# Regrouping the short matrix products of a chunked recurrence on TensorE

## The chip, the cores and the metric

The kernel runs on one core of one Trainium2 chip. The metric is the device time of one execution in microseconds (us); several runs of the same program are taken and their median is quoted. A profiled execution of the same program gives the trace.

## What is computed

One decoder layer over 256 tokens with a model width of 2048, all in f32:

```
h = rmsnorm(x);  u = h @ w_in          # ten column groups: c b xa za | q f iv og | ga gb
ya = b * conv3(c * xa) * silu(za)      # short convolution branch, 1024 wide
o  = hgrn2_chunked(silu(q), (1-lb)*sigmoid(-f), iv, log_f)   # 8 heads of 128
yb = rmsnorm_per_head(o) * silu(og)
m  = sigmoid(ga) * (ya @ w_a) + sigmoid(gb) * (yb @ w_b);  x = x + m @ w_o
x  = x + sigmoid(rmsnorm(x) @ w_pg) * (p @ w_pp);  out = rmsnorm(x)
```

The recurrence keeps a decaying state per head. For query time t and key time s <= t its weight is `sum_k q[t,k] * exp(B[t,k] - B[s,k]) * key[s,k]`, where B is the running sum of log_f. The result is these weights times the values `iv`.

## The kernel before, in words

**The main products.** The weights come from memory in chunks of 256 x 512 elements. Each chunk is split on the chip into a rounded half `whi` (ScalarE, ACT, line 124) and a remainder `wlo` (VectorE, DVE, line 125), and TensorE (PE) multiplies activations with them in three passes: 12 products of 128 x 128 by 512 columns per chunk (line 937, function `product`). There are four pairs of buffers `whi`/`wlo`, and the loop at line 940 splits up to four chunks ahead of the chunk being multiplied, so the split of chunk n waits until the products of chunk n-4 are done. Chunks are numbered from 0: 4 for `w_pp`, then 8 for each half of f, q, iv, og, c, xa, za, b, and so on.

**The epilogues.** What follows each group of columns is a Python generator. The main loop calls `advance()` once per chunk, which runs every active generator up to its next `yield`. A `yield` therefore puts what comes after it one chunk later. The program order of each engine is the order in which these pieces are issued, apart from small moves by the scheduler.

**The recurrence.** `hgrn(j)` (line 351) is such a generator, started once for each half j of the heads (4 heads of 128 channels) after the `og` columns. It covers 256 times as two blocks of 128, the second one held in reversed time order. In each block the 128 x 128 weights are built by levels: for block size B in `LEVELS = [128, 64, 32, 16, 8, 4]` the keys of one half of each block of B times meet the queries of the other half, with the decay split at the half's border. `level(B)` makes the decay factors with two subtractions (DVE and GpSimd), two exponentials (ACT), and `combine` makes the operand tile X with four multiplications (two on DVE, two on GpSimd, line 418). Then come:

- `products(bk, key, query, B)` (line 385): for each head, products on PE that use only a strip of the array's columns (`tile_position`). `quarters(B)` gives the strips: two of 64 rows for level 128, four of 32 rows for the others. They are f32, and each product is two instructions in the trace.
- `keep(dst, mask, src, B)` (line 394): masked copies (COPY_PREDICATED, line 396) from PSUM into the tile `both`, one for each strip.

Levels go two by two through two PSUM banks: products of two levels, then two yields, then the copies. After the third pair come the operands of the link between the two blocks (line 475 on), of the diagonal pairs (lines 488 to 501), and two masked copies of `both` into `a[:, 0]` and `a[:, 1]` (line 502). Then, in one burst on PE, the link `bo` (line 512, two strips of 64 rows, 128 columns) and the diagonal pairs of both blocks (line 519, through `products` with B = 2). Two chunks later DVE copies `bo` to `aoff` (line 522) and keeps the diagonals with four masked copies for each block (line 524); one chunk later PE multiplies `a` and `aoff` by the values (lines 529 to 532: 12 products of 128 x 128 by 128 columns, two instructions each).

So each half has five bursts of short products on PE among the main products: three of levels, one of link and diagonals, and the product with the values.

**The end.** `last_norm(1)` (line 756) scales the last 128 rows of the output in five pieces (DVE lines 770 and 776, ACT line 774) and sends each with a DMA (line 777), four of them from SyncE's queue (SP) and one from ACT's.

Of the kernel before, what the change touches and what calls it, by code (L numbers as in the profile page):

```python
# [11 lines left out]
AF = mybir.ActivationFunctionType  # L12
ALU = mybir.AluOpType
PSUM = bass.MemoryType.PSUM

P = 128
# [7 lines left out]
CW = 512  # L24
# [6 lines left out]
LEVELS = [128, 64, 32, 16, 8, 4]  # L31
# [13 lines left out]
def hybrid_kernel(ctx, tc, xT, x, pT, prm, gfin, masks, w_in, w_a, w_b, w_o, w_pg, w_pp, out):  # L45
    nc = tc.nc
# [124 lines left out]
    mask_t = const.tile([P, len(LEVELS) + 4, P], mybir.dt.int32, name="mask_t")  # L171
# [45 lines left out]
    def spread(ap, t):  # L217

        return ap.rearrange("p (b c t e) -> p t c b e", b=4, c=4, t=NT)[:, t]
# [128 lines left out]
    def hgrn(j):  # L351
# [9 lines left out]
        def new_X():  # L361

            n, made[0] = made[0], made[0] + 1
            X = t4("X", 2) if n % 4 < 2 else pools["branch"].tile(
                [P, 1024], F32, tag=f"ybT{'hl'[n % 2]}{j}", bufs=1, name=nm("X")
            )
            return X.rearrange("p (w h t) -> p w h t", w=2, h=4)

        a = tmp.tile([P, 2, 4, P], F32, tag="a", bufs=1, name=nm("a"))
        nc.gpsimd.memset(a, 0.0)  # L370
        both = tmp.tile([P, 4, P], F32, tag="both", bufs=1, name=nm("both"))
        nc.gpsimd.memset(both, 0.0)
        aoff = tmp.tile([P, 4, P], F32, tag="aoff", bufs=1, name=nm("aoff"))

        def heads(ap):
            return ap.rearrange("p (h t) -> p h t", h=4)

        def quarters(B):

            n = max(B // 2, 32)  # L380
            for r in range(P // n):
                c = r ^ 1 if B >= 64 else r
                yield slice(r * n, (r + 1) * n), slice(c * n, (c + 1) * n)

        def products(bk, key, query, B):

            for h in range(4):
                for r, c in quarters(B):
                    nc.tensor.matmul(  # L389
                        heads(bk)[r, h, c], key(h)[:, r], query(h)[:, c], start=True, stop=True,  # L390
                        tile_position=(0, r.start),
                    )

        def keep(dst, mask, src, B):
            for r, c in quarters(B):
                nc.vector.copy_predicated(  # L396
                    out=dst[r, :, c], data=src[r, :, c],
                    mask=mask_t[r, mask : mask + 1, c].to_broadcast([r.stop - r.start, 4, c.stop - c.start]),
                )

        def halves(ap, B):
            r = ap.rearrange("p (n two h) -> p n two h", two=2, h=B // 2)
            return r[:, :, 0, :], r[:, :, 1, :]
# [20 lines left out]
        def level(B):  # L424

            n, h = 1024 // B, B // 2
            e = t4()
            bl, br = halves(b, B)
            el, er = halves(e, B)
            if B > SCAN:  # L430
                nc.scalar.activation(out=el, in_=halves(y, B)[0], func=AF.Exp, scale=-1.0)
                nc.scalar.activation(out=er, in_=br, func=AF.Exp)
            else:
                ref = bl[:, :, h - 1 : h].to_broadcast([P, n, h])
                nc.vector.tensor_tensor(out=el, in0=bl, in1=ref, op=ALU.subtract)
                nc.gpsimd.tensor_tensor(out=er, in0=br, in1=ref, op=ALU.subtract)  # L436
                nc.scalar.activation(out=el, in_=el, func=AF.Exp, scale=-1.0)
                nc.scalar.activation(out=er, in_=er, func=AF.Exp)
            return combine(e, B)
# [4 lines left out]
            out=y.rearrange("p (n c) -> p n c", c=SCAN), in0=b.rearrange("p (n c) -> p n c", c=SCAN),  # L444
            in1=tot.rearrange("p (n o) -> p n o", o=1).to_broadcast([P, 16, SCAN]), op=ALU.subtract,
        )
        yield
        Xs = [level(LEVELS[0])]
        yield
        yield  # L450
        Xs.append(level(LEVELS[1]))
        yield
        yield
        yield

        for i in range(0, len(LEVELS), 2):
            bks = [bank("s") for _ in range(2)]
            for n, X in enumerate(Xs):
                products(bks[n], lambda h: X[:, 0, h, :], lambda h: X[:, 1, h, :], LEVELS[i + n])
            more = i + 2 < len(LEVELS)  # L460
            Xs = [level(LEVELS[i + 2])] if more else []
            yield
            yield
            for n, bk in enumerate(bks):
                keep(both, i + n, heads(bk), LEVELS[i + n])
            if more:
                Xs.append(level(LEVELS[i + 3]))
                yield
                yield
                yield  # L470

        e = t4()
        el, er = halves(e, P)
# [2 lines left out]
            out=el, in0=yl,  # L476
            in1=tot.rearrange("p (n s) -> p n s", s=2)[:, :, 1:2].to_broadcast([P, 8, SCAN]), op=ALU.subtract,
# [3 lines left out]
        X = new_X()  # L481
# [7 lines left out]
            out=f.rearrange("p (n c) -> p n c", c=1), in0=br, in1=bl, op=ALU.subtract  # L489
# [8 lines left out]
        for blk in range(2):  # L498
            kk, qq = k2[:, :, blk, :, 1 - blk, 0], q2[:, :, blk, :, 1 - blk, 0]
# [3 lines left out]
                out=a[:, blk],  # L503
                mask=mask_t[:, len(LEVELS) + blk : len(LEVELS) + blk + 1, :].to_broadcast([P, 4, P]), data=both,
# [2 lines left out]
        yield  # L507
        bo = bank("s")
        for h in range(4):
            for r in range(2):  # L510
                rows = slice(r * 64, (r + 1) * 64)
                nc.tensor.matmul(
                    heads(bo)[rows, h, :], X[:, 0, h, rows], X[:, 1, h, :], start=True, stop=True,
                    tile_position=(0, r * 64),
                )
        bk = [bank("s") for _ in range(2)]
        for blk in range(2):
            kk, qq = (z.rearrange("p (h k t) -> p h k t", h=4, k=2)[:, :, blk, :] for z in (kT, qT))
            products(bk[blk], lambda h: kk[:, h, :], lambda h: qq[:, h, :], 2)
        yield  # L520
        yield
        nc.vector.tensor_copy(out=aoff.rearrange("p h t -> p (h t)"), in_=bo)
        for blk in range(2):
            keep(a[:, blk], len(LEVELS) + 2 + blk, heads(bk[blk]), 2)
        yield
        o = [bank("s") for _ in range(2)]
        for h in range(4):
# [9 lines left out]
        for n in range(8):  # L537
            t, h = n // 4, n % 4
            if n == 4:
                yield  # L540
            nc.scalar.activation(
                out=sq[:, n * P : (n + 1) * P], in_=o[t][:, h * P : (h + 1) * P], func=AF.Square,
                scale=state["rstd1"][:, t : t + 1], accum_out=ss[:, n : n + 1],
            )
        for t in range(NT):
            s = slice(t * CW, (t + 1) * CW)
# [4 lines left out]
        for n in range(8):  # L551
            t, h = n // 4, n % 4
            if n == 4:
                yield
            nc.scalar.activation(
                out=spread(sq, t)[:, h], in_=yb[:, n * P : (n + 1) * P].rearrange("p (b e) -> p b e", e=32),
                func=AF.Identity, scale=rh[:, n : n + 1],
# [198 lines left out]
    def last_norm(t):  # L756

        xs, r, tot = state["x"], sc(1, "r3", 2), state["tot3", t]
        nc.vector.tensor_tensor(out=tot, in0=tot, in1=state["ss3"][:, t * 6 + 4 : t * 6 + 5], op=ALU.add)
        nc.gpsimd.tensor_tensor(out=r, in0=tot, in1=mhalf[:, :1], op=ALU.pow)  # L760
        n = CW // 2

        for eng, q0, q1, queue in (
            (nc.vector, 4, 5, nc.sync), (nc.vector, 5, 6, nc.sync), (nc.scalar, 0, 2, nc.sync),
            (nc.vector, 6, 8, nc.sync), (nc.scalar, 2, 4, nc.scalar),
        ):
            s = slice(q0 * n, q1 * n)
            d = xs[:, t, s]
            if q0 >= 6:
                nc.vector.scalar_tensor_tensor(  # L770
                    out=d, in0=d, scalar=r, in1=state["gfin"][:, s], op0=ALU.mult, op1=ALU.mult
                )
            elif eng is nc.scalar:
                nc.scalar.activation(out=d, in_=d, func=AF.Identity, scale=r)
            else:
                nc.vector.tensor_scalar(out=d, in0=d, scalar1=r, scalar2=None, op0=ALU.mult)
            queue.dma_start(out=out[:, t, s], in_=d)

    def ep_last(t, halves):

# [159 lines left out]
    for pos, (gi, c) in enumerate(steps[:last_group]):  # L940
        kind, j, w, g, opname = groups[gi]
# [35 lines left out]
        for i in range(2):  # L977
            k = 2 * c + i
            s = slice(i * CW, (i + 1) * CW)
# [41 lines left out]
    for t, halves in ((0, (0, 1)), (1, (0,)), (1, (1,))):  # L1021
        bk, n = bank("g"), CW // 2
        for c in range(nlast):
# [4 lines left out]
            for i in range(2):  # L1028
                k = 2 * c + i
                s = slice(i * CW + halves[0] * n, i * CW + (halves[-1] + 1) * n)  # L1030
# [85 lines left out]
```

## Time and profile before

| what | value |
|---|---|
| median of 3 runs | 831.42 us (831.42 to 831.85) |
| the profiled execution's own time | 831.84 us |
| its span in the trace | 830.1 us |
| PE busy (main and short products) | 816.9 us, 98% |
| DVE, ACT, GpSimd busy | 538.3, 430.9, 84.8 us |
| mean granted TensorE clock | 0.996 |

The trace gives each instruction's start and duration by engine and line. Matmuls are pipelined, so a PE row's duration overlaps with the next one's; the time that a product takes from the others is read from the distance between starts. Bursts of the first half lie between 123 and 186 us of the span, those of the second half between 307 and 370 us.

### The profile page before, as it was taken

Reading aid. Unit: us, or ns where it says so; the run is one execution under the profiler, and the core shown is the slowest. Engines: PE = TensorE matmul, PEld = TensorE weight load, DVE = VectorE, ACT = ScalarE, POOL = GpSimd, SP = SyncE. Lnnn points to the kernel's source line nnn. Section 1 sums busy time; section 2 is a strip of 40 time slices with the busy share of each in tenths; the row PEclk is TensorE's granted clock in tenths of the full one; section 3 lists DMA queues with packets and bytes.
Section 4 is the critical chain, followed back from the end, with each engine's and each line's share of the span. In section 5 each row is a group of like instructions: output and inputs, shape, how many; then the busy total and the mean of one; then the engine's idle time right before and its main releaser. Section 6 shows DMA issues by size and latency. Waiting matters only on the chain.

```text
span 830.1 us, 10589 instructions
## 1 busy us (share of the span) xinstructions
PE 816.9 (98%) x4122; PEld 674.3 (81%) x4122; DVE 538.3 (65%) x662; ACT 430.9 (52%) x553; POOL 84.8 (10%) x74
## 2 busy tenths in 40 slices
PE   9999999999999999999999999999999999999995
PEld 6888888878888888878888888888888888888885
DVE  6746678896866588896745545545645656679633
ACT  7666565446564465455544443443444455566522
POOL 1000035110000054100001001000100000001210
PEclk9999999999999999999999999999999999999998
DMA  9969655647876554657655755755655787987702
GB/s 341 372 256 340 222 193 197 204 153 219 277 235 232 203 203 152 204 192 241 227 203 172 254 189 196 253 203 191 231 191 198 253 281 246 330 304 269 293 0 103
DMA packets 40947, 187.25 MB, mean 226 GB/s; under 512 B 4672, under 2 KB 14400, under 8 KB 22720
## 3 DMA queue, kind: packets, MB, share of 16 engines
q1 hardware_dynamic: 40464, 185.78, 64.7%
q10 hardware_dynamic: 432, 0.79, 0.3%
q8 instruction: 32, 0.52, 0.3%
q14 instruction: 19, 0.16, 0.1%
HBM read 172.92 MB, written 13.63 MB: 225 GB/s over the span
## 4 chain that ended last, share of the span: by engine, by line
PE 93%; DVE 3%; issue 2%; ACT 1%; POOLq 0%; POOL 0%; DVEq 0%
PE g L937 91%; DVE wlo L125 1%; PE s L389 1%; PE s L937 1%; PE s L817 1%; DVE t L264 0%; PE s L531 0%; PE s L529 0%; DVE a L396 0%; ACT whi L124 0%; DVE both L396 0%; DVE X L483 0%; PE s L530 0%; DVE t L492 0%; DVE t L494 0%
## 5 line engine op out<-in xcount | busy, mean ns | idle before, releaser
L125 DVE TENSOR_TENSOR wlo<-raw,whi 128x1024 fp32r<-128x1024 f32 (+1 forms) x293 | 360.4, 1235 | 251.8 <-ACT whi L124 250.8
L124 ACT ACTIVATE whi<-raw 128x1024 fp32r<-128x1024 f32 (+1 forms) x293 | 307.6, 1056 | 323.6 <-PE g L937 279.4
L937 PE MATMUL g<-whi,xh 128*128 128x512 f32 (+1 forms) x912 | 352.0, 387 | 0.0
L937 PE MATMUL g<-whi,xl 128*128 128x512 f32 (+1 forms) x912 | 351.8, 386 | 0.0
L937 PE MATMUL g<-wlo,xh 128*128 128x512 f32 (+1 forms) x912 | 351.7, 386 | 0.0
L937 PEld LDWEIGHTS g<-whi,xh 128*128 128x128 f32 x912 | 171.3, 188 | 34.6
L937 PEld LDWEIGHTS g<-whi,xl 128*128 128x128 f32 x912 | 171.3, 188 | 34.3
L937 PEld LDWEIGHTS g<-wlo,xh 128*128 128x128 f32 x912 | 171.4, 188 | 33.9
L937 PE MATMUL g<-whi,mh 128*128 128x512 f32 x128 | 49.8, 390 | 0.0
L937 PE MATMUL g<-wlo,mh 128*128 128x512 f32 x128 | 49.7, 389 | 0.0
L937 PE MATMUL g<-whi,ml 128*128 128x512 f32 x128 | 49.6, 390 | 0.0
L659 POOL TENSOR_TENSOR t<-ga,gb 128x512 f32<-128x512 f32 x6 | 10.6, 1786 | 195.8 <-DVE gb L654 195.8
L937 PE MATMUL g<-whi,yaTh 128*128 128x512 f32 x72 | 28.3, 399 | 0.0
L937 PEld LDWEIGHTS g<-whi,mh 128*128 128x128 f32 x128 | 24.0, 188 | 5.3 <-ACT mh L665 0.3
L937 PE MATMUL g<-whi,yaTl 128*128 128x512 f32 x72 | 28.3, 396 | 0.0
L937 PEld LDWEIGHTS g<-whi,ml 128*128 128x128 f32 x128 | 23.9, 188 | 5.1 <-DVE ml L666 0.2
L937 PEld LDWEIGHTS g<-wlo,mh 128*128 128x128 f32 x128 | 24.0, 188 | 5.0
L937 PE MATMUL g<-wlo,yaTh 128*128 128x512 f32 x72 | 27.9, 390 | 0.0
L436 POOL TENSOR_TENSOR t<-b 128x512 f32<-128x512 f32 x10 | 18.9, 1890 | 67.0 <-DVE b L319 38.7
L937 PE MATMUL g<-whi,ybTh 128*128 128x512 f32 x64 | 24.9, 389 | 0.0
L937 PE MATMUL g<-whi,ybTl 128*128 128x512 f32 x64 | 24.9, 389 | 0.0
L937 PE MATMUL g<-wlo,ybTh 128*128 128x512 f32 x64 | 24.9, 389 | 0.0
(154 smaller groups left out, 522.4 us busy)
## 6 DMA issues: line engine op xcount, KB each, us to landing
raw<-in_w_in SPq DMA_DIRECT2D x93, 1024.0 KB, 5.0
raw<-in_w_o SPq DMA_DIRECT2D x16, 1024.0 KB, 5.5
raw<-in_w_pg SPq DMA_DIRECT2D x16, 1024.0 KB, 5.8
turn<-t SPq DMA_DIRECT2D x72, 128.0 KB, 2.7
t<-turn SPq DMA_DIRECT2D x18, 512.0 KB, 4.9
raw<-in_w_a SPq DMA_DIRECT2D x8, 1024.0 KB, 5.0
raw<-in_w_b SPq DMA_DIRECT2D x8, 1024.0 KB, 5.0
raw<-in_w_in SPq DMA_DIRECT2D x6, 512.0 KB, 8.3
```

The lines of the kernel that those rows point to most:

```text
L124: a = nc.scalar.activation(out=hi[:, s], in_=src[:, s], func=AF.Copy)
L125: v = nc.vector.tensor_tensor(out=lo[:, s], in0=src[:, s], in1=hi[:, s].bitcast(F32), op=ALU.subtract)
L389: nc.tensor.matmul(heads(bk)[r, h, c], key(h)[:, r], query(h)[:, c], start=True, stop=True, tile_position=(0, r.start),)
L436: nc.gpsimd.tensor_tensor(out=er, in0=br, in1=ref, op=ALU.subtract)
L659: (nc.vector if j == 3 else nc.gpsimd).tensor_tensor(out=spread(m, t), in0=blocks(ga[:, s]), in1=blocks(gb[:, s]), op=ALU.add)
L817: nc.tensor.matmul(wb, warm[:, :P], warm, start=True, stop=True)
L937: nc.tensor.matmul(psum, a, b, start=first and n == 0, stop=last and n == 2)
```

## The change

- `quarters(B)` now yields four strips of 32 rows at every level; level 128 has 64 columns in each.
- The narrow levels 32, 16, 8, 4 are made first. Their products go in one burst into one PSUM bank, level i at columns 32*i of each head's 128. Four masked copies of the full 128 x 512 follow, each reading its 32 columns repeated over the four column blocks.
- The wide levels 128 and 64 are made after that burst. Their products are issued with the link and the diagonals, in the same bank as the first block's diagonal; the second block's diagonal takes 32 columns of another bank.
- The link's products use four strips of 32 rows instead of two of 64, and its copy `aoff` goes from DVE to ACT.
- The two masks for the shared bank are put together from the loaded ones by four small DVE instructions in the first half.
- Three masked copies of 128 x 512 take the place of the eight after the diagonals. There are two yields in place of one before the product with the values. In all, the product with the values of each half stands one chunk earlier than before (behind chunk 60 in place of three products into chunk 62 in the first half, by the built program).
- `last_norm` works in four pieces of 512 columns in place of five.

```diff
         def quarters(B):
-            n = max(B // 2, 32)
-            for r in range(P // n):
-                c = r ^ 1 if B >= 64 else r
-                yield slice(r * n, (r + 1) * n), slice(c * n, (c + 1) * n)
-
-        def products(bk, key, query, B):
+            for r in range(0, P, 32):
+                c = {128: (r // 64 ^ 1) * 64, 64: r ^ 32}.get(B, r)
+                n = max(B // 2, 32)
+                yield slice(r, r + 32), slice(c, c + n)
+
+        def products(bk, key, query, B, at=None):
             for h in range(4):
                 for r, c in quarters(B):
                     nc.tensor.matmul(
-                        heads(bk)[r, h, c], key(h)[:, r], query(h)[:, c], start=True, stop=True,
-                        tile_position=(0, r.start),
+                        heads(bk)[r, h, c if at is None else slice(at, at + 32)], key(h)[:, r], query(h)[:, c],
+                        start=True, stop=True, tile_position=(0, r.start),
                     )
-        def keep(dst, mask, src, B):
-            for r, c in quarters(B):
+        def keep(dst, mask, src, at=None):
+            if at is None:
                 nc.vector.copy_predicated(
-                    out=dst[r, :, c], data=src[r, :, c],
-                    mask=mask_t[r, mask : mask + 1, c].to_broadcast([r.stop - r.start, 4, c.stop - c.start]),
+                    out=dst, data=src, mask=mask_t[:, mask : mask + 1, :].to_broadcast([P, 4, P])
                 )
+                return
+            n = P // 32
+            nc.vector.copy_predicated(
+                out=dst.rearrange("p h (n c) -> p h n c", n=n),
+                data=src[:, :, at : at + 32].rearrange("p h (n c) -> p h n c", n=1).to_broadcast([P, 4, n, 32]),
+                mask=mask_t[:, mask : mask + 1, :].rearrange("p h (n c) -> p h n c", n=n).to_broadcast([P, 4, n, 32]),
+            )
...
         yield
-        Xs = [level(LEVELS[0])]
-        yield
-        yield
-        Xs.append(level(LEVELS[1]))
-        yield
-        yield
-        yield
-
-        for i in range(0, len(LEVELS), 2):
-            bks = [bank("s") for _ in range(2)]
-            for n, X in enumerate(Xs):
-                products(bks[n], lambda h: X[:, 0, h, :], lambda h: X[:, 1, h, :], LEVELS[i + n])
-            more = i + 2 < len(LEVELS)
-            Xs = [level(LEVELS[i + 2])] if more else []
+        if j == 0:
+            m = lambda i: mask_t[:, i, :]
+            for out, a0, a1, op in ((0, 0, 1, ALU.max), (1, 0, 7, ALU.mult), (0, 0, 6, ALU.mult), (0, 0, 8, ALU.max)):
+                nc.vector.tensor_tensor(out=m(out), in0=m(a0), in1=m(a1), op=op)
+        Xs = []
+        for i in range(2, len(LEVELS)):
+            Xs.append(level(LEVELS[i]))
             yield
             yield
-            for n, bk in enumerate(bks):
-                keep(both, i + n, heads(bk), LEVELS[i + n])
-            if more:
-                Xs.append(level(LEVELS[i + 3]))
+            if i % 2:
                 yield
-                yield
-                yield
+        bk = bank("s")
+        for i, X in enumerate(Xs):
+            products(bk, lambda h: X[:, 0, h, :], lambda h: X[:, 1, h, :], LEVELS[2 + i], 32 * i)
+        Xs = [level(LEVELS[0])]
+        yield
+        yield
+        for i in range(4):
+            keep(both, 2 + i, heads(bk), 32 * i)
+        Xs.append(level(LEVELS[1]))
+        yield
+        yield
+        yield
...
         bo = bank("s")
         for h in range(4):
-            for r in range(2):
-                rows = slice(r * 64, (r + 1) * 64)
+            for r in range(0, P, 32):
                 nc.tensor.matmul(
-                    heads(bo)[rows, h, :], X[:, 0, h, rows], X[:, 1, h, :], start=True, stop=True,
-                    tile_position=(0, r * 64),
+                    heads(bo)[r : r + 32, h, :], X[:, 0, h, r : r + 32], X[:, 1, h, :], start=True, stop=True,
+                    tile_position=(0, r),
                 )
         bk = [bank("s") for _ in range(2)]
+        for i, X in enumerate(Xs):
+            products(bk[0], lambda h: X[:, 0, h, :], lambda h: X[:, 1, h, :], LEVELS[i])
         for blk in range(2):
             kk, qq = (z.rearrange("p (h k t) -> p h k t", h=4, k=2)[:, :, blk, :] for z in (kT, qT))
-            products(bk[blk], lambda h: kk[:, h, :], lambda h: qq[:, h, :], 2)
-        yield
-        yield
-        nc.vector.tensor_copy(out=aoff.rearrange("p h t -> p (h t)"), in_=bo)
-        for blk in range(2):
-            keep(a[:, blk], len(LEVELS) + 2 + blk, heads(bk[blk]), 2)
+            products(bk[blk], lambda h: kk[:, h, :], lambda h: qq[:, h, :], 2, 0 if blk else None)
+        yield
+        yield
+        nc.scalar.activation(out=aoff.rearrange("p h t -> p (h t)"), in_=bo, func=AF.Copy)
+        keep(a[:, 0], 0, heads(bk[0]))
+        keep(a[:, 1], 1, heads(bk[0]))
+        keep(a[:, 1], len(LEVELS) + 3, heads(bk[1]), 0)
+        yield
         yield
...
     def last_norm(t):
-        n = CW // 2
-        for eng, q0, q1, queue in (
-            (nc.vector, 4, 5, nc.sync), (nc.vector, 5, 6, nc.sync), (nc.scalar, 0, 2, nc.sync),
-            (nc.vector, 6, 8, nc.sync), (nc.scalar, 2, 4, nc.scalar),
-        ):
-            s = slice(q0 * n, q1 * n)
+        for q in (2, 0, 3, 1):
+            s = slice(q * CW, (q + 1) * CW)
             d = xs[:, t, s]
...
-            queue.dma_start(out=out[:, t, s], in_=d)
+            (nc.scalar if q == 1 else nc.sync).dma_start(out=out[:, t, s], in_=d)
```

More of the change, by code (lines that the diff above doesn't have):

```diff
@@ L760, in last_norm @@
         nc.gpsimd.tensor_tensor(out=r, in0=tot, in1=mhalf[:, :1], op=ALU.pow)
-        n = CW // 2
-        for eng, q0, q1, queue in (
-            (nc.vector, 4, 5, nc.sync), (nc.vector, 5, 6, nc.sync), (nc.scalar, 0, 2, nc.sync),
-            (nc.vector, 6, 8, nc.sync), (nc.scalar, 2, 4, nc.scalar),
-        ):
-            s = slice(q0 * n, q1 * n)
-            d = xs[:, t, s]
-            if q0 >= 6:
+        for q in (2, 0, 3, 1):
+            s = slice(q * CW, (q + 1) * CW)
+            d = xs[:, t, s]
+            if q < 2:
+                nc.scalar.activation(out=d, in_=d, func=AF.Identity, scale=r)
+            elif q == 2:
+                nc.vector.tensor_scalar(out=d, in0=d, scalar1=r, scalar2=None, op0=ALU.mult)
+            else:
                 nc.vector.scalar_tensor_tensor(
@@ L772, in last_norm @@
                 )
[L773 to L777, printed above, removed]
+            (nc.scalar if q == 1 else nc.sync).dma_start(out=out[:, t, s], in_=d)
     def ep_last(t, halves):
```

## The prediction

> **What bounds the kernel now.** I read the page first, then the waits of PE, then the chain of work that ended last.
>
> ```profile
> span 830.1 us, 10589 instructions
> PE 816.9 (98%) x4122; PEld 674.3 (81%) x4122; DVE 538.3 (65%) x662; ACT 430.9 (52%) x553; POOL 84.8 (10%) x74
> ...
> PE 93%; DVE 3%; issue 2%; ACT 1%; POOLq 0%; POOL 0%; DVEq 0%
> ...
> L125 DVE TENSOR_TENSOR wlo<-raw,whi 128x1024 fp32r<-128x1024 f32 (+1 forms) x293 | 360.4, 1235 | 251.8 <-ACT whi L124 250.8
> L124 ACT ACTIVATE whi<-raw 128x1024 fp32r<-128x1024 f32 (+1 forms) x293 | 307.6, 1056 | 323.6 <-PE g L937 279.4
> ```
> ```profile
> PE s L529 <- DVE a L396: 2.6, 2, 1.3
> ```
> ```profile
> 185.35 121.77 PE g L937 x537
> ```
>
> PE is the bound: it is 98% busy and makes 93% of the chain. The splits on ACT and DVE wait for it (279.4 us of ACT's idle time), not it for them. In the second fence, once the kernel runs, PE waits for another engine in one place only, the product with the values (line 529), once for each half. The third row gives the pace: 121.77 us for 537 products, 0.227 us each. So whatever is taken out of PE's stream between two main products comes off the end, one for one, as long as nothing else becomes late. What counts is how much longer than 0.227 us the main products stand apart around the short ones.
>
> **The bursts.** The timeline of PE in the first half, one block for the first pair of levels, one for the second, the ends of one for the third, one for link and diagonals, one for the product with the values (columns: start, length, what, count):
>
> ```profile
> 123.05 0.39 PE L937 MATMUL g<-whi,xl 128*128 128x512 f32 x1
> 123.37 1.07 PE L389 MATMUL s<-X 128*64 128x64 f32 x48
> 124.37 0.50 PE L937 MATMUL g<-whi,xh 128*128 128x512 f32 x1
> 124.71 0.40 PE L937 MATMUL g<-wlo,xh 128*128 128x512 f32 x1
> ...
> 137.86 0.39 PE L937 MATMUL g<-whi,xl 128*128 128x512 f32 x1
> 138.18 0.77 PE L389 MATMUL s<-X 128*32 128x32 f32 x64
> 139.21 0.40 PE L937 MATMUL g<-wlo,xh 128*128 128x512 f32 x1
> ...
> 152.40 0.39 PE L937 MATMUL g<-whi,xl 128*128 128x512 f32 x1
> ...
> 153.75 0.40 PE L937 MATMUL g<-wlo,xh 128*128 128x512 f32 x1
> ...
> 169.66 0.39 PE L937 MATMUL g<-whi,xl 128*128 128x512 f32 x1
> 169.98 1.09 PE L512 MATMUL s<-X 128*64 128x128 f32 x16
> 171.00 0.76 PE L389 MATMUL s<-qT,kT 128*32 128x32 f32 x64
> 171.70 0.50 PE L937 MATMUL g<-whi,xh 128*128 128x512 f32 x1
> 172.03 0.40 PE L937 MATMUL g<-wlo,xh 128*128 128x512 f32 x1
> ...
> 180.44 0.39 PE L937 MATMUL g<-whi,xl 128*128 128x512 f32 x1
> 182.13 0.46 PE L529 MATMUL s<-v,a 128*128 128x128 f32 x2 [1.30 <-DVE a L396]
> 184.06 0.39 PE L530 MATMUL s<-v,aoff 128*128 128x128 f32 x2
> 184.29 0.39 PE L531 MATMUL s<-v,a 128*128 128x128 f32 x2
> 185.10 0.48 PE L937 MATMUL g<-whi,xh 128*128 128x512 f32 x1
> 185.42 0.40 PE L937 MATMUL g<-wlo,xh 128*128 128x512 f32 x1
> ```
>
> The first main product after a burst also holds up the second (0.34 us), so I measure from the last main product before to the second one after, less two paces (0.453 us). Burst 1 costs 1.66 - 0.453 = 1.21 us, burst 2 1.35 - 0.453 = 0.90, burst 3 (levels 8 and 4) 0.90, link with diagonals 2.37 - 0.453 = 1.92: together 4.92 us a half. The product with the values costs 4.98 - 0.453 = 4.53.
>
> How much of it is work? Two narrow windows inside bursts 2 and 1:
>
> ```profile
> 138.24 0.39 PE L389 MATMUL s<-X 128*32 128x32 f32 x25
> ```
> ```profile
> 123.48 0.40 PE L389 MATMUL s<-X 128*64 128x64 f32 x7
> ```
>
> A row's length runs to the end of its last instruction, and one lasts about 0.2 us here, so 25 instructions of 32 columns start within 0.2 us: 0.0079 us each. Those of level 128 start 7 in 0.18 us: 0.029 us each. Burst 2 is then 64 x 0.0079 = 0.51 us of work and 0.39 us of entering and leaving. That 0.39 is what a removed burst saves. Changing the strip's width inside a burst costs too: burst 1 is 0.39 + 32 x 0.0079 + 16 x 0.029 = 1.10, 0.11 under what it took.
>
> After the change a half has burst A, four narrow levels: 128 x 0.0079 + 0.39 = 1.40 us. Burst B has link, wide levels and diagonals. Its work is that of burst 4 (1.92, entering and leaving included) and of burst 1 without its fixed part (1.21 - 0.39 = 0.82): 2.74 us with both changes of width kept, about 2.50 if these vanish because all strips are now 32 wide. The unknown is a strip of 32 with long rows, which this trace does not hold: level 128 and the link become 32 instructions each in place of 16. I take four strips side by side at half the cost of two, as the 32-column rows run (0.0079 against 0.029 for twice the columns and twice the width, near a quarter). So A and B are 3.90 to 4.14 against 4.92: 0.8 to 1.0 us saved a half, and I take 1.0. The bound above is no gain from four strips over two, 16 more instructions of each kind at today's cost: 16 x 0.029 = 0.46 for the level, and for the link 16 x 0.055 = 0.88 (its 16 take 1.02 us before the diagonals start, less the change of width). The bound below is the short rows' 0.0079 for all 64, some 0.8 us cheaper; that would need rows two and four times as long to cost nothing, so I leave it out.
>
> The Trainium skill speaks against many small products: "TensorE: Matmul & The Clock Gate", in the section that asks why 56 ns and not 53.3, says that starts never come closer than about 25 ns however few the columns. By it the 32 added instructions would cost 0.8 us a half and the sum would be 827.7 us. The row with 25 starts in 0.2 us does not agree: separate strips start three times closer than that, so I give this case no chance of its own.
>
> **The wait before the product with the values.** Its clean cost is 24 instructions at 0.111 us (two rows of x2 stand 0.23 us apart), 2.68 us, and 0.09 us on each side (the burst's first start comes 0.32 after a main product in place of 0.227): 2.86 us. The other 1.67 of the 4.53 us is waiting, mostly the 1.46 us from 180.67 to 182.13. What ended it, from DVE's timeline:
>
> ```profile
> 177.72 1.41 DVE L264 SCALAR_TENSOR_TENSOR t<-g,r1s,t 128x512 f32<-128x512 f32 x2
> 179.04 1.22 DVE L125 TENSOR_TENSOR wlo<-raw,whi 128x1024 fp32r<-128x1024 f32 x1
> 180.18 0.69 DVE L522 COPY aoff<-s 128x512 f32<-128x512 f32 x1
> 180.78 2.46 DVE L396 COPY_PREDICATED a<-mask_t,s 32x128 f32<-32x128 int32 x8
> ```
>
> The copies stand behind the split of chunk 63, the product with the values three products into chunk 62. Split 63 cannot begin before product 59 ends. From there two chunks and three products (6.1 us) hold a split (1.06 + 1.23), `aoff` (0.6) and the copies (2.46), 0.8 us to spare, and the `za` work on line 264 (1.41) in front of the split eats it.
>
> In the built program the three copies stand behind the split of chunk 61 and the product with the values behind chunk 60. Split 61 can begin when product 57 ends, three chunks (8.2 us) ahead. In that time DVE needs the split's 2.3 us, the copies and one convolution step (0.35). The `za` work now follows them, and `aoff` is on ACT, behind split 61 and in front of split 62. For the copies:
>
> ```profile
> L396 DVE COPY_PREDICATED both<-mask_t,s 32x128 f32<-32x128 int32 x40 | 12.0, 299 | 0.8
> L396 DVE COPY_PREDICATED a<-mask_t,s 32x128 f32<-32x128 int32 x16 | 4.7, 294 | 0.2
> L502 DVE COPY_PREDICATED a<-mask_t,both 128x512 f32<-128x512 int32 x4 | 3.0, 762 | 0.0
> L396 DVE COPY_PREDICATED both<-mask_t,s 64x256 f32<-64x256 int32 x4 | 1.8, 446 | 0.0
> ```
>
> From 128 to 256 columns a copy grows by 0.147 us, so 512 cost about 0.75, which the row of line 502 confirms. Three of them make 2.3 us. Of 8.2 us 3.3 are left, so the wait goes: 1.67 us a half. DVE as a whole gets lighter: (12.0 + 4.7 + 1.8) / 2 = 9.3 us of copies a half become 7 x 0.76 = 5.3, and `aoff` leaves it. The four mask instructions (128 columns each, about 0.3 us, once) come early, where split buffers are four chunks deep. Repeated reading of 32 columns in PSUM is a pattern not in this trace; I price it by its 512 columns, and bound it by twice that. At 1.5 us a copy DVE would reach the diagonal's keys 3 us later. By my walk along its queue they are ready 1.8 us before burst B wants them, so PE would wait 1.2 us a half. What is late next is DVE still: level 128 reuses the buffer of level 32, so its multiplications wait for burst A; the splits behind them are for chunks that PE reaches three chunks later.
>
> **The end.**
>
> ```profile
> 823.52 0.62 DVE L776 TENSOR_SCALAR xs<-xs,r 128x256 f32<-128x256 f32 x2 [0.67 <-POOL r L760]
> 823.90 2.06 SPq L777 DMA_DIRECT2D out<-xs  x4
> ```
>
> SP issues four DMAs about 0.55 us apart ((2.06 - 0.41) / 3, the last lasting 0.41), the last at 825.55. With one piece for the first two, the first leaves 0.27 us later (when 0.62 us of scaling is done) and the last of three at 824.17 + 1.10 = 825.27, 0.28 us earlier. If the transfers set the end it is up to 0.27 later. I take 0.15 earlier.
>
> **The sum.** 2 x (1.0 + 1.67) + 0.15 = 5.5 us. Against the profiled execution's own 831.84 us (span 830.1 and 1.7 around it) that gives 826.3 us; against the median of 831.42 it gives 825.9. I predict 826.1 us.
>
> **The rivals.**
> - *The wait stays.* DVE falls behind through the four wide copies and the `za` work, and PE waits as long as before, at the same product or in burst B. Against it are the 3.3 us to spare; for it, DVE has run behind PE at this place in both halves. Then 2 x 1.0 + 0.15 are saved: 829.5 us.
> - *Long strips run two at a time.* The link and level 128 cost 0.88 + 0.46 more a half, 2.7 in all: 828.8 us. For it: no row of long 32-wide strips exists here.
> - *The entering and leaving does not go with the burst but with the number of levels.* Then only waits and the end are saved, 3.5 us: 828.1 us. Against it: burst 4 changes operands with no visible gap inside its 64 diagonal rows. The Trainium skill, "TensorEngine Tiling (Array Packing)", key properties, says that changing the tiling mode, not just the tile, drains the array. By that it goes with the burst, and the 0.39 us agree.
> - *Slower: long strips run one at a time.* At the full-width 0.111 us for each of the link's 32 instructions and half of that for the level's, burst B grows by 32 x (0.111 - 0.0275) + 32 x (0.055 - 0.0145) = 4.0 us a half: 826.1 + 8.0 = 834.1 us. It decides once burst B takes over 5.2 us in place of 2.5. Against it, the 64-wide ones ran two at a time.
>
> **How the numbers follow.** Forecast 0.70, its own range 824.6 to 827.4 (0.25 us a half for the width changes, 0.4 for the end, 0.4 between runs, and some of the wait kept). Wait stays 0.10, two at a time 0.08, fixed cost stays 0.07, one at a time 0.03, something unseen 0.02. The range 824.6 to 829.0 takes in the forecast, two at a time and the fixed cost, and leaves out the rest. About 0.2%, 1.7 us, can be told from no change: faster is under 829.8. All cases but the last two are faster, and the wait case stands near that border: faster 0.93, same 0.03, slower 0.04.
>
> **What would show it.** In the profile after: two stretches of short products a half before the product with the values, about 1.4 and 2.5 us by the distance of main products; no wait of PE at the product with the values, which takes 2.9 us; copies of 512 columns near 0.76 us; SP's last output DMA 0.3 us nearer to the scaling. It is wrong if burst B takes 4 us or more, or if a wait on DVE shows in PE's list with 1 us or more a half.

## The result

| | before | after |
|---|---|---|
| median of 4 runs | 831.52 us (831.42 to 831.85) | 826.38 us (826.25 to 827.48) |
| profiled execution: own time, span | 831.84, 830.1 us | 827.48, 825.0 us |

The ratio is 0.994, 95% interval 0.9923 to 0.9958: faster by 5.1 us, against a forecast of 826.1 us. The profiled execution of after is the slowest of its four; the spans of the others are 824.5 to 824.7.

The page of after, its span, engines and chain:

```profile
span 825.0 us, 10664 instructions
PE 814.1 (99%) x4186; PEld 674.1 (82%) x4186; DVE 533.1 (65%) x616; ACT 431.6 (52%) x555; POOL 86.8 (11%) x74
...
PE 96%; issue 1%; DMA 1%; DVE 0%; ACT 0%; SPq 0%; POOLq 0%; POOL 0%
```

PE is still the bound, and DVE has left the chain (3% before). PE's list of waits holds the warm-up and one line more:

```profile
PE s L825 <- DVE warm L821: 1.2, 1, 1.2
PE g L945 <- issue: 0.5, 1, 0.5
```

The wait for DVE's copies is gone. In its place stands something new, a wait for "issue", that is for nothing that the profile shows, at a main product. PE's timeline of after, first half, shows where: burst A, burst B and what follows it, then the product with the values (start, length, what, count):

```profile
136.50 0.39 PE L945 MATMUL g<-whi,xl 128*128 128x512 f32 x1
136.82 1.36 PE L389 MATMUL s<-X 128*32 128x32 f32 x128
138.11 0.50 PE L945 MATMUL g<-whi,xh 128*128 128x512 f32 x1
138.45 0.40 PE L945 MATMUL g<-wlo,xh 128*128 128x512 f32 x1
...
162.52 0.39 PE L945 MATMUL g<-whi,xl 128*128 128x512 f32 x1
162.84 1.08 PE L520 MATMUL s<-X 128*32 128x128 f32 x32
163.74 0.93 PE L389 MATMUL s<-X 128*32 128x64 f32 x64
164.51 0.75 PE L389 MATMUL s<-qT,kT 128*32 128x32 f32 x64
165.20 0.50 PE L945 MATMUL g<-whi,xh 128*128 128x512 f32 x1
165.54 0.40 PE L945 MATMUL g<-wlo,xh 128*128 128x512 f32 x1
...
166.48 0.39 PE L945 MATMUL g<-whi,xl 128*128 128x512 f32 x1
167.41 0.50 PE L945 MATMUL g<-whi,xh 128*128 128x512 f32 x1 [0.54 <-issue]
167.74 0.40 PE L945 MATMUL g<-wlo,xh 128*128 128x512 f32 x1
...
176.86 0.39 PE L945 MATMUL g<-whi,xl 128*128 128x512 f32 x1
177.09 0.38 PE L542 MATMUL s<-v,a 128*128 128x128 f32 x2
...
179.68 0.48 PE L945 MATMUL g<-whi,xh 128*128 128x512 f32 x1
179.99 0.40 PE L945 MATMUL g<-wlo,xh 128*128 128x512 f32 x1
```

By the prediction's own measure (last main product before to the second one after, less 0.453 us): burst A 1.49, burst B 2.56, values 2.68 us. Together 6.73 a half, against 9.45 before; the second half reads the same to 0.01 us. That saves 2.72 a half, 5.43 in all. Between 166.48 and 167.74 the same measure gives 0.81 us in which PE stands still with no short product near, in the first half only.

The whole difference of spans is 5.05 us, and it can be laid out by stretches. Between the 100th main product and the 2000th lie 449.87 us before and 445.21 after, 4.67 less (5.43 less the stop of 0.81 is 4.62). Another 0.15 is in the first 29 us, where profiles of all the kernels here scatter between 28.5 and 29.2, so that this share means nothing. The last 0.24 is behind the last main product (9.57 us, then 9.33).

### The profile page after: what moved, and what is told of

Read it like the earlier page. It is cut to its first block, busy times and chain, and to the rows that moved or that the text cites. A ratio compares the mean times of both kernels' runs of the same rounds, so it can differ in the third digit from the quotient of the medians.

```text
span 825.0 us, 10664 instructions
## 1 busy us (share of the span) xinstructions
PE 814.1 (99%) x4186; PEld 674.1 (82%) x4186; DVE 533.1 (65%) x616; ACT 431.6 (52%) x555; POOL 86.8 (11%) x74
## 4 chain that ended last, share of the span: by engine, by line
PE 96%; issue 1%; DMA 1%; DVE 0%; ACT 0%; SPq 0%; POOLq 0%; POOL 0%
PE g L945 94%; PE s L945 1%; PE s L389 1%; DMA raw<-in_w_pp 1%; PE s L520 0%; PE s L544 0%; PE s L543 0%; PE s L542 0%; ACT xs L778 0%; DVE wlo L125 0%; ACT whi L124 0%; DVE t L748 0%; DVE t L752 0%; DVE xs L751 0%; POOLq L1119 0%
## 5 line engine op out<-in xcount | busy, mean ns | idle before, releaser
L125 DVE TENSOR_TENSOR wlo<-raw,whi 128x1024 fp32r<-128x1024 f32 (+1 forms) x293 | 365.5, 1253 | 252.3 <-ACT whi L124 251.5
```

The costliest lines, as they stand in the source:

```text
L125: v = nc.vector.tensor_tensor(out=lo[:, s], in0=src[:, s], in1=hi[:, s].bitcast(F32), op=ALU.subtract)
```

## The experiments

Time is the median; the stretch of PE in which the reason shows is given with it. Runs of one series were taken on one chip. A place is the position of an instruction in PE's program, where each product counts as two (its weights, then the product).

**The wait by itself.** The kernel before, with a `yield` more:

```
         yield
+        yield
         o = [bank("s") for _ in range(2)]
```

> The kernel before with one more yield ahead of the product with the values, so that it stands behind chunk 61's split by one chunk more; bursts, copies and the end stay as they were. Theory 1 (distance): the copies and aoff get 2.7 us more, the 1.67 us of waiting per half goes, the product with the values takes 2.7 to 2.9 us by the distance of main products in place of 4.53, and the time falls by 3.3 us, to 828.2. Rival (DVE itself is late, the many small copies hold it): a good part of the wait stays, the time falls by less than 1.5 us. The four bursts stay at 1.20, 0.89, 0.89 and 1.92 us in either case.

Measured 828.61 us (828.54 to 828.70) against 831.86 in the same series, 3.25 less; ratio 0.9961 (0.9946 to 0.9976). PE's timeline at the product with the values, and above it the copies on DVE:

```profile
180.72 2.49 DVE L396 COPY_PREDICATED a<-mask_t,s 32x128 f32<-32x128 int32 x8
```
```profile
182.41 0.39 PE L938 MATMUL g<-whi,xl 128*128 128x512 f32 x1
182.64 0.38 PE L530 MATMUL s<-v,a 128*128 128x128 f32 x2
182.86 0.39 PE L531 MATMUL s<-v,aoff 128*128 128x128 f32 x2
183.26 0.49 PE L532 MATMUL s<-v,a 128*128 128x128 f32 x2
...
185.52 0.47 PE L938 MATMUL g<-whi,xh 128*128 128x512 f32 x1
```

The copies end at 183.21, and the third product starts at 183.26, 0.4 us after the one ahead of it where 0.22 is the pace: a remainder of the wait. The stretch takes 2.97 us, 1.56 less than before, and the bursts stay as they were. So distance in the program alone takes nearly all of the wait away, as theory 1 had it (2.7 to 2.9 us expected for the stretch).

**One chunk less in after.** The same line, taken out of the kernel after:

```
         keep(a[:, 1], len(LEVELS) + 3, heads(bk[1]), 0)
         yield
-        yield
```

> The kernel after with one yield in place of two between the last masked copies and the product with the values, which so comes one chunk (2.72 us) earlier. Theory 1 (distance): of the 2.64 us in which DVE stood idle ahead of the split of chunk 61, and the time by which the copies were early, some 3 us were to spare; one chunk less leaves about 0.4, so the product with the values takes 2.7 to 3.2 us and the time is 0 to 1.0 us above the kernel after. Rival (the wide copies and aoff on ACT removed the wait, the extra chunk was not needed): no change at all in that place, 2.68 us. Rival (the chunk was all of it): the wait of 1.67 us is back in both halves, 3.3 us slower, 829.7.

Measured 826.56 us (826.04 to 826.72), and the values take 2.68 us: no wait. The last copy and the first product with the values, in this kernel:

```profile
172.83 0.73 DVE L402 COPY_PREDICATED a<-mask_t,s 128x512 f32<-128x512 int32 x1
```
```profile
174.26 0.38 PE L541 MATMUL s<-v,a 128*128 128x128 f32 x2
```

The copy ends at 173.56, 0.7 us before that product starts. Theory 1 had given a margin of about 0.4. But the outcome is what the first rival named: the second chunk of distance is not needed in this kernel, and what else the change does is enough too. Between the two kernels DVE lost `aoff` (0.68), some 0.4 us of copies and the `za` work (1.41) ahead of the values; which of them decides was not tried apart.

**Where TensorE stops: two shifts.** A stop with no releaser, in one half of two equal ones, is a reason to look at how the instructions themselves arrive. The page of after has a DMA queue for them:

```profile
q8 instruction: 32, 0.52, 0.2%
```

32 packets bring 16 KB each, one for every 262 of PE's 8372 recorded instructions. Main products use up a block in about 29 us (128 products with their weight loads at 0.227 us). Burst A has 256 instructions in 1.5 us and burst B 320 in 2.6. The trace has a packet starting at 164.98 that takes 0.96 us; 1.47 us after its landing PE runs again. The Trainium skill, "Runtime: NRT & Kernel Launch", section on instruction fetch mechanics, says that instructions come in 16 KiB blocks of 256; the trace agrees. To move the borders, the warm-up was cut into more pieces:

```
-    for _ in range(WARM):
-        nc.tensor.matmul(wb, warm[:, :P], warm, start=True, stop=True)
+    for _ in range(63):                     # or 40, with 128 columns
+        nc.tensor.matmul(wb[:, :80], warm[:, :P], warm[:, :80], start=True, stop=True)
```

> The kernel after with 63 warm-up products of 80 columns in place of 10 of 512: about as much TensorE work ahead of the first main product, but 106 more instructions, so that every later instruction of TensorE lies 106 places further in the program. Theory F (the stop of 0.81 us six main products after burst B of the first half is TensorE without instructions: its instruction queue brings blocks of 16 KB, 256 instructions, two block borders lie at 76 and 332 places from the start of that burst, and the second is reached 2.6 us after the first where a block takes about 3.5 us): the borders now lie 30 places before that burst and 226 into it, over 5 us apart, and in the other bursts no pair is closer than that. No stop in any place, bursts unchanged (1.49, 2.56, 2.68), 0.8 us faster than the kernel after: 825.6. Rival G (the stop belongs to the place or the moment, whatever the numbering): it stays at 0.8 us behind burst B of the first half, and the time stays at 826.4.

> The kernel after with 40 warm-up products of 128 columns in place of 10 of 512: 60 more instructions ahead of everything. Theory F: the block borders lie 16 and 272 places into burst B of the first half, which is passed in about 1.85 us where a block takes 3.5. The stop moves into the burst, to its diagonal products, and grows to about 1.65 us, so that burst B takes 4.2 us in the first half and 2.56 in the second; nothing stands still behind it. Time 0.8 us above the kernel after: 827.2. Rival G: 0.8 us behind burst B as before, 826.4.

Measured 826.30 us (826.17 to 826.34) and 826.02 (825.94 to 826.39). No stop in either behind burst B; bursts and values unchanged. From the 100th main product to the 2000th both take 444.3 us, 0.9 less than the profile of after above and 0.4 to 0.5 less than its two later ones. The times alone would not show it: after took 826.38 in another series, and 825.6 was expected with 106 places. Theory F was right that numbering decides and wrong on how: with 60 places it had the stop growing to 1.65 us. In that run the packet starts at 160.05, 2.9 us ahead of burst B's first product. So a block is asked for earlier than one block ahead of its use: about 306 places by these runs (F2). The later profiles bear this out: in the twelve of after and its variants, no packet of this queue starts more than 306 places ahead of the border that it serves, taking packets and borders in order.

**F2 tested.** The next four are one series. First the kernel after again, then 16 places (18 products of 284 columns):

> The kernel after, unchanged, beside the next three. Theory F2 (TensorE's instruction blocks, corrected by the two shifted runs: a block of 256 instructions is asked for some 306 places ahead of the place where TensorE needs it, and takes 3.9 to 4.3 us; it comes too late where those 306 places are passed in less): the stop stands six main products behind burst B of the first half again, 0.4 to 0.8 us, and nowhere else; time 826.5. Rival H (a disturbance of single runs): no stop, or one in another place.

> The kernel after with 18 warm-up products of 284 columns in place of 10 of 512, 16 more instructions of TensorE ahead of everything. Theory F2: the block that was asked for 26 places into burst B of the first half and needed 332 places from its start is now asked for at 10 and needed at 316, four instructions ahead of the burst's end. The 306 places take 2.2 us there in place of 3.4, so the stop moves to the burst's very end and grows to 1.7 to 2.1 us: the distance of main products over burst B is 4.3 to 4.7 us in the first half (2.67 in the second), and behind it there is no stop. About 1.2 us slower than the kernel after. Rival H (any other warm-up removes the stop, as 60 and 106 places did): none anywhere, 0.4 to 0.8 us faster than the kernel after.

The kernel after took 827.12 us (826.73 to 827.39), and its profile has the stop at the same product, 0.42 us. With 16 places it took 827.91 (827.53 to 828.30). PE's timeline and list of waits in that run:

```profile
163.06 1.08 PE L520 MATMUL s<-X 128*32 128x128 f32 x32
163.96 0.93 PE L389 MATMUL s<-X 128*32 128x64 f32 x64
164.73 0.74 PE L389 MATMUL s<-qT,kT 128*32 128x32 f32 x62
167.35 0.25 PE L389 MATMUL s<-qT,kT 128*32 128x32 f32 x2 [1.89 <-issue]
167.53 0.50 PE L945 MATMUL g<-whi,xh 128*128 128x512 f32 x1
```
```profile
PE s L389 <- issue: 1.9, 1, 1.9
```

158 of the burst's 160 products run, which is 316 instructions, and then PE stops for 2.1 us: the place named to the instruction, and the burst takes 4.68 us in place of 2.56 (4.3 to 4.7 expected). Rival H falls, since here another warm-up makes it worse.

**Strips of 64 rows again** for the link and, with `quarters` as it was before, for level 128:

```
-            for r in range(0, P, 32):
+            for r in range(0, P, 64):
                 nc.tensor.matmul(
-                    heads(bo)[r : r + 32, h, :], X[:, 0, h, r : r + 32], X[:, 1, h, :], ...
+                    heads(bo)[r : r + 64, h, :], X[:, 0, h, r : r + 64], X[:, 1, h, :], ...
```

> The kernel after with the link and level 128 in strips of 64 rows again (half as many products, two strips side by side); bursts and banks as after. Theory 1 (four strips of 32 run in half the time of two of 64, and changes of width cost 0.11 to 0.14 each): the link's 32 instructions become 16 at 0.055, 0.88 us, those of level 128 16 at 0.029, 0.46, against the 0.87 and 0.44 that they take after; with one change of width burst B takes 0.05 to 0.25 us a half more than its 2.56. Theory F2: burst B is 64 instructions shorter, the place where the late block is needed lies 76 places behind its end, and the stop goes, 0.4 to 0.8 us. Sum: within 0.6 us of the kernel after, either way. Rival (narrower strips bring nothing, the width changes neither): burst B stays within 0.03 us of 2.56.

826.39 us (826.33 to 826.64), 0.7 less than the kernel after in this series. PE's timeline, to be read against the three rows of burst B in after:

```profile
162.99 1.09 PE L520 MATMUL s<-X 128*64 128x128 f32 x16
163.91 1.02 PE L389 MATMUL s<-X 128*64 128x64 f32 x48
164.75 0.80 PE L389 MATMUL s<-qT,kT 128*32 128x32 f32 x64
165.48 0.50 PE L945 MATMUL g<-whi,xh 128*128 128x512 f32 x1
```

The link takes as long with 16 instructions as with 32 (0.92 and 0.90 us from its start to that of the next row). Burst B takes 2.69 us, 0.13 more a half, and the stop is gone. So narrow strips bring 0.13 us a half here, and with 64 instructions more they bring the stop; at this numbering they cost more than they bring.

**The old end** (five pieces and four DMAs on SP):

> The kernel after with the end of the kernel before: five pieces of output, four DMAs on SP for each of the last rows in place of three. Theory 1 (the issue of the last DMA on SP sets the end): from the last main product to the span's end 9.6 us in place of 9.33, 0.28 us slower; bursts and values unchanged. Rival (the transfers set it): 0 to 0.27 us faster than after.

826.62 us (826.59 to 827.03). SP's issues of the output:

```profile
818.83 2.17 SPq L790 DMA_DIRECT2D out<-xs  x4
```
```profile
819.22 1.55 SPq L785 DMA_DIRECT2D out<-xs  x3
```

The first is the old end, the second the kernel after. Counted from the last main product (815.41 and 815.67 us), the last issue leaves 0.29 us earlier in after (5.06 and 4.77 us). But the span ends only 0.05 us earlier: 9.39 against 9.33 to 9.35 in three profiles of after. Both expectations miss; most of the earlier issue does not reach the end. Even the 0.05 is small beside the scatter: other kernels with the new end show 9.18 to 9.37, the two others with the old one 9.56 and 9.57. The median is 0.5 us below that of the kernel after in this series, which the end does not explain.

**Burst A in two, and burst A twice as long.**

```
         for i, X in enumerate(Xs):
+            if i == 2:
+                yield
```
```
-        for i, X in enumerate(Xs):
+        for i, X in enumerate(Xs + Xs):
+            i = i % 4
```

> The kernel after with burst A in two: levels 32 and 16 first, one chunk later levels 8 and 4, into the same bank. Theory 1 (entering and leaving costs 0.39 us a burst, a level of narrow strips 64 places 32 instructions at 0.0079 to 0.0086): two stretches of 0.89 to 0.95 us in place of one of 1.49, 0.39 us more a half, 0.8 us in all, and burst B as it was. Rival (the fixed cost goes with the levels): the two stretches together take what the one did, 1.49, and the time stays.

> The kernel after with every product of burst A made twice (the same values written again), so that the burst has 512 instructions of TensorE in place of 256. Theory 1 (0.0086 us an instruction of 32 columns, as burst A's 1.49 less 0.39 over 128 gives): 1.1 us more a half for the work. Theory F2 on top of it (a block is needed 306 places behind the place where it is asked for, and takes 3.9 to 4.3 us): in the first half the block asked for 14 places ahead of the burst is needed 292 places into it, 3.0 us later, so the burst stops for 0.9 to 1.3 us and takes 3.5 to 3.9 us by the distance of main products; in the second half the block asked for at 130 is needed at 436, about 1.5 us later, so it stops for 2.4 to 2.8 us and takes 5.0 to 5.4 us. Rival (no start closer than 25 ns): 3.2 us more for the work in both halves alike, evenly spread over the products. Rival (no law of blocks): 2.6 us in both halves.

Split, PE's timeline of the two halves of burst A, and of burst B:

```profile
136.80 0.76 PE L389 MATMUL s<-X 128*32 128x32 f32 x64
...
140.42 0.76 PE L389 MATMUL s<-X 128*32 128x32 f32 x64
...
167.47 0.70 PE L389 MATMUL s<-qT,kT 128*32 128x32 f32 x58
169.54 0.26 PE L389 MATMUL s<-qT,kT 128*32 128x32 f32 x6 [1.37 <-issue]
```

Each half takes 0.90 us by the distance of main products, 1.80 together against 1.49. Entering and leaving is thus 0.31 us, and it goes with the burst. That the time rose by more (828.61 us, 827.76 to 829.75) has a second reason, which the expectation had overlooked: with a chunk between the halves burst B begins 12 main products (24 instructions) later in the program, so the border of the block lies at 332 - 24 = 308 places. The stop stands there, behind 154 products, and costs 1.58 us. The two reasons make 2 x 0.31 + 1.58 - 0.51 = 1.7 us over the kernel after with its own stop (0.51, below); measured in the same series are 1.8.

Twice, one run of 836.66 us:

```profile
137.38 1.51 PE L389 MATMUL s<-X 128*32 128x32 f32 x147
141.72 1.19 PE L389 MATMUL s<-X 128*32 128x32 f32 x109 [2.83 <-issue]
...
323.24 2.12 PE L389 MATMUL s<-X 128*32 128x32 f32 x217
327.73 0.55 PE L389 MATMUL s<-X 128*32 128x32 f32 x39 [2.37 <-issue]
328.21 0.64 PE L946 MATMUL g<-whi,xh 128*128 128x512 f32 x1
```

The stops come behind 147 and 217 products, 294 and 434 instructions, where 292 and 436 were expected; the second burst takes 5.27 us (5.0 to 5.4 expected). The first takes 5.66 us where 3.5 to 3.9 was expected: its packet starts at 139.45, 2.1 us into the burst. So the place follows from the borders. F2's size holds in the second half and fails in the first, where the packet starts late; why is open. The 25-ns rival falls with the first row: 147 products start within about 1.3 us, 9 ns each.

**The kernel after beside the one with 60 places.**

> The kernel after, unchanged, beside shift60_again on one chip. Theory F2: the stop six main products behind burst B of the first half, 0.4 to 0.8 us, as in the two profiles of it so far; 826.4 to 827.1 us.

> The kernel after with 40 warm-up products of 128 columns (60 more instructions ahead of everything), again, beside the kernel after on one chip. Theory F2: no stop, 0.4 to 0.8 us faster than the kernel after in the same minutes. Rival (run-to-run differences at the start of the kernel are as large): within 0.2 us of it.

The kernel after 826.83 us (826.30 to 827.33), ratio to before 0.994 (0.9928 to 0.9953). With 60 places 826.23 (825.64 to 826.42), ratio 0.9932 (0.9918 to 0.9945). The medians stand 0.6 us apart, as expected, though the ranges touch. The profiles tell it more sharply: a stop of 0.51 us at the same product in the one, none in the other. By medians, the version with 60 places is the fastest on record (826.02 and 826.23).

## Why the prediction was right, point by point

The forecast held (826.1 against 826.38), and its mechanism with it: the wait went, and fewer bursts cost less. That the figure came so near is partly luck, since two errors of opposite sign lie in it: the gains were 0.2 to 0.3 us larger than forecast, and a stop that nothing in the forecast held took 0.8 us of them in the profile.

- *The wait.* Right: 4.53 us became 2.68, where 2.86 was forecast. The clean cost is 24 products at 0.111 and hardly anything at the sides, so 1.85 us a half were saved and not 1.67. Distance alone removes 1.56 of it (the first experiment). On DVE the split of chunk 61 starts at 170.25, the copies behind it, and the product with the values comes at 177.09:

```profile
170.25 1.23 DVE L125 TENSOR_TENSOR wlo<-raw,whi 128x1024 fp32r<-128x1024 f32 x1 [2.64 <-ACT whi L124]
171.40 1.36 DVE L397 COPY_PREDICATED a<-mask_t,s 128x512 f32<-128x512 int32 x2
...
172.89 0.75 DVE L402 COPY_PREDICATED a<-mask_t,s 128x512 f32<-128x512 int32 x1
```

  The copies end 3.4 us ahead of it (3.3 to spare had been forecast).
- *Bursts.* A 1.49 in place of 1.40, B 2.56 in place of 2.50, so 0.87 saved a half in place of 1.0. The terms mis-sized are the fixed part, 0.31 us in place of 0.39, and the narrow instruction: (1.49 - 0.31) / 128 = 0.0092 in place of 0.0079, which came from too narrow a window. The prediction's own row of burst 2 gives the larger figure: 64 products in 0.77 us, the last one 0.2 long, are (0.77 - 0.2) / 63 = 0.0090. The two errors cancel for 64 products, from which they were read; for 128 they leave 0.09 us. Long strips do run four at a time: the link's 32 take 0.90 us, 0.028 each, where 0.0275 was assumed. That refutes both rivals on long strips.
- *The fixed cost goes with the levels*: refuted by the split burst, which pays 0.31 us once more for entering and leaving. The drain at a change of tiling mode that the prediction quoted from the Trainium skill, "TensorEngine Tiling (Array Packing)", key properties, agrees with this.
- *The copies*:

```profile
L402 DVE COPY_PREDICATED both<-mask_t,s 128x512 f32<-128x512 int32 x8 | 6.0, 750 | 0.0
L459 DVE TENSOR_TENSOR mask_t<-mask_t 128x128 int32<-128x128 int32 x4 | 2.6, 658 | 0.0
```

  0.750 us for 512 columns read repeatedly (0.75 forecast). The four mask instructions take 0.66 each, twice the 0.3 forecast; they are hidden as it said.
- *The end*: 0.15 forecast, 0.24 between the two profiles, of which the experiment gives the new pieces 0.05. Both lie inside its bounds; the rest lies within the scatter between profiles or is not explained.
- *The sum.* Waits and bursts 5.43 in place of 5.34, the end 0.24, the start 0.15 that was not in the sum and is scatter. That would be 5.8 us. What it lacked is the stop, 0.4 to 0.8 us in the five profiles of kernels that share after's numbering up to burst B (after three times, the old end, one chunk less). With 60 or 106 places more and no stop, 826.0 to 826.3 us were measured, the forecast's figure. No rival named it: the prediction looked at engines, buffers and transfers, and took for granted that PE has its next instruction.

## What to carry to other kernels

Measure a burst of short products from main product to main product: its price is 0.3 us for entering and leaving plus the products, so fewer, longer bursts pay, as long as TensorE does not run out of instructions in them: here bursts of 256 instructions never did, one of 320 did at some numberings and one of 512 in both halves. A stop of TensorE with "issue" as its releaser, in one of two equal halves, is read from the instruction queue: count instructions up to it, and shift the numbering to test it. Where a wait can be removed by distance in the program, try that alone: one `yield` brought 3.25 of the 5.1 us.

## What the runs showed of the hardware that was not expected

TensorE can run out of instructions. In these runs it stops at the border of a block of 256 instructions that has not arrived. In seven profiles (after three times, the old end, one chunk less, 16 places, burst A in two) the product that waits is the 989th that PE's record holds, whether it is a main product or one inside a burst. PE runs again 1.2 to 1.6 us after the packet has landed (ten stops in eight profiles). The stops were 0.4 to 0.8 us in the kernel after and those with its numbering, and once more there in the doubled one (0.78), 1.6 and 2.1 us with the border at 308 and 316 places, and 2.4 to 2.8 us (the profile's idle time) in the doubled burst.

Two things have to be kept apart. The places follow from the border in after and the 256 alone: three were named ahead of their runs to within two instructions, the fourth, 308, was worked out afterwards. The 306 of F2 says when a block is asked for, and so how long the stop is. The request itself is not in the trace, so the 306 is a fit; it gave two of the three sizes named for other kernels (4.3 to 4.7 and 5.0 to 5.4 us, measured 4.68 and 5.27) and missed one (3.5 to 3.9, measured 5.66).

The Trainium skill, "Runtime: NRT & Kernel Launch", section on instruction fetch mechanics, has such fetches hidden for the most part behind the pace at which instructions are issued. That holds for the main products here, and at some numberings not for a burst of 320 instructions in 2.6 us.

After the stop of 2.4 us in the doubled burst's second half the clock fell as well. The windows of that run behind it, and the next (span, PE and its count, weight loads, the other engines, granted clock):

```profile
328.20:331.60 3.40, 3.40 (x14) 2.64 (x9) 0.00 (x0) 0.00 (x0) 0.00 (x0) 0.53 0.47 195
331.60:335.00 3.40, 3.40 (x16) 2.80 (x15) 1.05 (x1) 1.58 (x2) 0.49 (x1) 0.97 0.00 0
```

For 3.4 us the granted clock was 0.53, and main products started 0.43 us apart in place of 0.227. After the 2.8 us stop of the first half it stayed at 1.00, so the length of a stop alone doesn't decide.
